# Other places in SBUF for the operands of three matmul stages of a decoder layer

## The chip, the cores and the metric

The kernel runs on one core of one Trainium2 chip. The metric is the device time of one execution in microseconds. TensorE (PE) does the matmuls, VectorE (DVE), ScalarE (ACT) and GpSimd (POOL) the elementwise work, and SyncE (SP) issues most transfers. All operands of a matmul lie in SBUF, each in 128 partitions, and a tile is a stretch of bytes that has the same place in every partition.

## The reference

One hybrid decoder layer over 16 meta tokens and 1,024 tokens of width 1,024: a joint input projection, differential attention and an HGRN2 recurrence side by side, an output projection, and a convolutional FFN with 2 x 2,816 channels.

```python
a = rmsnorm(h, ln_mix_pre[l])
proj = a @ w_in[l]
dq, dk, dv, hq, hf, hi, hg = jnp.split(proj, SPLITS, axis=-1)
y_diff = diff_attention(dq, dk, dv, ...)
y_hgrn = hgrn2(hq, hf, hi, hg, lb_all[l], hgrn_gnorm[l])
mix = jnp.concatenate([y_diff, y_hgrn], axis=-1) @ w_out[l]
h = h + rmsnorm(mix, ln_mix_post[l])
a = rmsnorm(h, ln_ffn_pre[l])
y = conv_ffn(a, w_ffn_up[l], ffn_conv_w[l], ffn_conv_b[l], w_ffn_down[l])
h = h + rmsnorm(y, ln_ffn_post[l])
```

`conv_ffn` is `u = a @ w_up`, a causal depthwise convolution of width 3 over the tokens, `gelu(gate) * up`, and `@ w_down`. Everything is float32.

## The kernel before, in words

A float32 product is made of three fp32r matmuls. Each operand is split into a high part (rounded to fp32r) and a low part (the rest), and hi x hi, hi x lo and lo x hi are summed in PSUM. A matmul has a stationary tile of 128 x 128, which TensorE loads for it, and a streamed operand of up to 512 columns. The load for one matmul runs while the one before it streams. TensorE's instructions stand in the order in which the code issues them (`manual_schedule`).

Three stages matter here.

The *projections* (`proj_step`, L243, and the class `Kinds`, L892) have weights stationary (`wh`, `wl`) and stream the normalized activations `ahi` and `alo`, tiles of 8 x 1,152 columns, over three groups of token blocks: 272, 384 and 384 columns. `place(t)` (L46) says at which column a token stands; after the first group it leaves 16 columns (64 bytes) free. `gap(...)` takes some bytes that nobody uses, so that the tiles behind it move up. The projections of one head run between the small matmuls of attention or HGRN of another.

The *up stage* (`unit`, L1396) uses one level of Strassen's scheme in Winograd's form: per 128 channels seven products `mm(0)` to `mm(6)`, each over four blocks of 128 rows and for two parts of the tokens, p = 0 with 258 columns and p = 1 with 256. The weights `uh`, `ul` are stationary. The streamed tiles `t0_0` to `t0_6` and `t1_0` to `t1_6` are made once, before the loop, by `t_split` and `t_sums`; each holds four high blocks and then four low ones. L1411 streams the high block against high weights, L1412 the low block against high weights, L1413 the high block against low weights. A block of 258 columns is 1,032 bytes long, so the low half starts 4,128 bytes behind the high one, which is 32 bytes modulo 512, and each next block 8 bytes further modulo 512; with 256 columns (1,024 bytes) all blocks of a tile have one place modulo 512. The loop over `ft` runs the 258-wide and the 256-wide product of each j in turn, 12 matmuls each, 21 times seven. The first unit (`plain_unit`, L1378) does without Strassen and uses four of the tiles.

The *down stage* (`operands`, L1500, `mms`, L1580) also has seven products. Here the gated activations are stationary: `gh` and `gl`, tiles of 512 columns in a ring of four buffers each (pool `down`), of which matmul m takes columns 128 m to 128 m + 127. The weights `wh`, `wl` (512 columns) are streamed: L1585 `wh` against `gh`, L1586 `wl` against `gh`, L1587 `wh` against `gl`. Each step of a product takes one buffer of each and does 12 matmuls, three for each of four PSUM banks.

The output projection between them streams weights too (L1031 to L1035), against tiles of the mixed heads; the tile `m7` holds the eighth row block, whose products have `pz` as output where they are added last (`out_last`, L1081).

All weight tiles, `wh` and `wl` of every stage, stand at 480 modulo 512 in each of their buffers, but for the third projection's first tiles (`w3`, taken from the attention's pool).

Of the kernel before, what the change touches and what calls it, by code (L numbers as in the profile page):

```python
# [9 lines left out]
F32 = mybir.dt.float32  # L10
F32R = mybir.dt.float32r
# [6 lines left out]
P = 128  # L18
# [19 lines left out]
def start(i):  # L38
    return 0 if i == 0 else META + P * (i - 1)
# [4 lines left out]


def place(t):  # L46
    return t + (0 if t < start(3) else 16)


class Ordered:  # L50
# [40 lines left out]
def layer_kernel(ctx: ExitStack, tc: tile.TileContext, x, meta, table, lbl, gpre, gpost, win,  # L91
# [7 lines left out]
    def pool(name, bufs, side="left", space=None):  # L99
        kw = {"side": side} if space is None else {"space": space}  # L100
        cm = tc.tile_pool(name=name, bufs=bufs, reuse_waits="tile", **kw)
        return cm, cm.__enter__()
# [70 lines left out]
    mx_cm, mxp = pool("mix", 1)  # L173

    MIX = {"X0": 2064, "X1": 2176, "X2": 2080}
# [4 lines left out]
    def gap(where, name, n):  # L180
        where.tile([P, n // 4], F32, tag=name, name=name, bufs=1)
# [11 lines left out]
                         m[:, l, off:off + P * n].bitcast(F32).rearrange("p (b c) -> p b c", c=P))  # L193

    at_cm, atp = pool("at", 1)
    gap(atp, "edge", 64)
    ahi, alo = (atp.tile([P, KD, P * NBLK], F32R, tag=t, name=t) for t in ("ahi", "alo"))

    last_load, lows = [], []
# [837 lines left out]
    def meta_part(py, wo, full):  # L1037
        for k in range(KD - 1):
            hi, lo = wo[k]
            both = [(34, hi), (2, lo)]  # L1040
            if k == KD - 2:
                both.reverse()
            for i, (r, w) in enumerate(both):
                T.matmul(py[:r], m0[:, 2 * k:2 * k + r], w, start=(k == 0 and i == 0), stop=(r == 34 and k == KD - 2))
                yield 216
            if k == 0 and full:
                yield from out_part(m0_7, py, wo[KD - 1:], range(1), False, False)
# [18 lines left out]
    def second_load(i):  # L1066
        blocks[i] = block_tile(1, i)
        block_load(blocks[i], i, 0, 4)
        block_load(blocks[i], i, 4, 7 if i == 1 else 8)
# [7 lines left out]
    def y0_gain(p):  # L1077
        r = tok(p)[0]
        return G.tensor_tensor(y0[:r, p], y0[:r, p], gpo0[:r], op=ALU.mult)
# [40 lines left out]
    def ps_b(name):  # L1120
        return pp.tile([P, 512], F32, tag="b", name=name)
# [80 lines left out]
    def load_xh(i):  # L1202
        r = tok(i)[0]
        if i:
            xhs[i] = qp.tile([P, D], F32, tag="xh", name=f"xh{i}")
        else:
            xhs[i], xhs["sum"] = xh0[:, :D], xh0[:, D:]
        SY.dma_start(xhs[i][:r], meta[14:16, :] if i == 0 else x[P * (i - 1): P * i, :])
# [51 lines left out]
    def t_tiles(p, j, where, tag):  # L1260
        tag, n, off = (tag + (8 * WN[p], 0)[len(tag) - 1:])[:3]
        both = where.tile([P, n], F32R, tag=tag, name=f"t{p}_{j}")[:, off:off + 8 * WN[p]].rearrange("p (a c) -> p a c", a=8)
        return both[:, 0:4], both[:, 4:8]

    def t_split(p, j, src, where, *tag):
        hi, lo = t_tiles(p, j, where, tag)
        marks["cast"] = A.copy(hi, src)
        marks["low"] = V.tensor_tensor(lo, src, hi.bitcast(F32), op=ALU.subtract)
        tt[p][j] = (hi, lo)

    def quarter(p, j):
        n = WN[p]
        a, c = {0: (0, 0), 7: (0, n), 4: (4, 0), 6: (4, n)}[j]
        return at2[p][:, a:a + 4, c:c + n]

    def t_sums(p, where, last):
        b11, b12, b21, b22 = (quarter(p, j) for j in (0, 7, 4, 6))
        cast, low = marks["quarters"]
        with tc.issue_after(low.ins) if p else nullcontext():
            V.tensor_tensor(b11, b12, b11, op=ALU.subtract)  # L1280
        V.tensor_tensor(b12, b22, b12, op=ALU.subtract)
        V.tensor_tensor(b22, b22, b11, op=ALU.subtract)
        for j, b in ((1, b22), (2, b11), (3, b12)):
            if p == 0:
                gap(where, f"gap4{j}", 128 if j == 1 else 192)
            with nullcontext() if p or j == 1 else tc.issue_after(cast.ins):
                with nullcontext() if p or j == 1 else tc.issue_after(low.ins):
                    t_split(p, j, b, where, f"t{p}_{j}")
        V.tensor_tensor(b21, b21, b22, op=ALU.subtract)
        with nullcontext() if p else tc.issue_after(cast.ins):  # L1290
            with nullcontext() if p else tc.issue_after(low.ins):
                t_split(p, 5, b21, *last)

    def run(*args):
        for _ in out_part(*args):
            pass
# [4 lines left out]
    for i in range(1, NBLK):  # L1301
        py = ps_b(f"py1_{i}")
        if i >= 3:
            marks["gain"] = y0_gain(i)
        if i == 1:
            load_xh(1)
            load_xh(0)
        if i + 1 < NBLK:
            for n in range(i + 1 if i < 6 else i + 2, min(i + 2 if i < 5 else i + 3, NBLK)):
                second_load(n)  # L1310
            load_xh(i + 1)
        run(blocks[i], py, wo, range(4), True, False)
        if i == 3:
            trans(1)
        run(blocks[i], py, wo, range(4, 7 if i == 1 else 8), False, i > 1)
        if i > 3:
            trans(i - 2)
        if i == 5:
            trans(0)
        if i == 1:  # L1320
            pm = ps_b("py1_0")
            for _ in meta_part(pm, wo, True):
                pass
            for p in range(3):
                out_last(p)
            run(k7(1), py, wo[KD - 1:], range(1), False, True)
            post(1, py)
            ysum = xhs.pop("sum")
            for l in range(2):
                A.copy(ysum[:2, 512 * l:512 * l + 512], pm[32 * l:32 * l + 2])  # L1330
            G.tensor_tensor(ysum[:2, :512], ysum[:2, :512], ysum[:2, 512:], op=ALU.add)
            for p in (3, 4):
                out_last(p)
            continue
        post(i, py)
        if i == 2:
            post(0, ysum[:, :512], ysum[:, 512:])
        if i == 5:
            t_split(0, 0, quarter(0, 0), ep, "e0")
            t_split(0, 4, quarter(0, 4), ep, "e1")  # L1340
        if i == 7:
            with tc.issue_after(marks["scale"].ins), tc.issue_after(marks["normed"].ins):
                t_split(0, 7, quarter(0, 7), mxp, "X2", MIX["X2"])
        if i == 8:
            t_split(0, 6, quarter(0, 6), mxp, "X1", MIX["X1"], 16)
        if i in (2, 3):
            for p in (1 + 2 * i, 2 + 2 * i):
                out_last(p)
# [6 lines left out]
    def outputs(ft, p):  # L1355
        if ft == 1 or ft and ft % 2 == NF % 2:
            if p == 0:
                return [dn.tile([P, 2 * WN[0]], F32, tag="gk", name=f"{t}{ft}_{p}") for t in ("ug", "uu")]
            return [dn.tile([P, 512], F32R, tag=g, name=f"{t}{ft}_{p}").bitcast(F32) for g, t in (("gh", "ug"), ("gl", "uu"))]
        return [xup.tile([P, 2 * WN[0]], F32, tag=t, name=f"{t}{ft}_{p}") for t in ("ug", "uu")]  # L1360

    def conv(ft, p, side, u):
# [94 lines left out]
    t_sums(0, tp, (mxp, "X2", MIX["X2"], 16))  # L1457
    close(a_cms.pop())
    t2_cm, t2p = pool("tsplit2", 1)
    gap(t2p, "gap2", 64)  # L1460
    p1 = plain_unit(1, ps_b)
    for j in range(4):
        with tc.issue_after(wo_low[5].ins), tc.issue_after(wo_low[4].ins):
# [6 lines left out]
    dn_cm, dn = pool("down", 4, "right")  # L1470
# [29 lines left out]
    def operands(pr, k, loaded=None):  # L1500
        ga, gb, gc, gs = (keep[nm][:, k] if keep else None for nm in ("ga", "gb", "gc", "gs"))
        if pr == 1:
            a = loaded[0] if loaded else g_in(k, 0, "1")
        elif pr == 2:
            SY.dma_start(gb, g_src(k + NH, 0))
            a = gb
        elif pr == 5:
            a = gs
        elif pr == 6:
            V.tensor_tensor(gs, gs, ga, op=ALU.add)  # L1510
            a = gs
        elif pr == 3:
            V.tensor_tensor(gb, gs, gb, op=ALU.subtract)
            a = gb
        elif pr == 7:
            V.tensor_tensor(ga, gc, ga, op=ALU.subtract)
            a = ga
        else:
            a = g_in(k + NH, 1, "4")
        b = loaded[1] if loaded else w_in(pr, k)  # L1520
        nm = f"{pr}_{k}"
        gh = dn.tile([P, 512], F32R, tag="gh", name=f"gh{nm}")
        gl = dn.tile([P, 512], F32R, tag="gl", name=f"gl{nm}")
        split(gh, gl, a, V)
        wh = wp.tile([P, 512], F32R, tag="wh", name=f"wh{nm}", bufs=4)
        wl = wp.tile([P, 512], F32R, tag="wl", name=f"wl{nm}", bufs=4)
        split(wh, wl, b, V)
        return gh, gl, wh, wl
# [210 lines left out]
```

## Time and profile before

| | us |
|---|---|
| median of the runs | 1275.93 (1275.89 to 1275.97) |
| profiled execution, whole | 1276.64 |
| its span, first to last instruction | 1274.9 |
| projections, attention, HGRN | from the start to 497 |
| output projection, residual, norm | 497 to 617 |
| first FFN unit | 617 to 643 |
| up stage | 643 to 1055 |
| down stage and tail | 1055 to the end |

The page and the views give, for a group of instructions, its source line, engine, operation and tiles, written out<-in without buffer numbers, how many there are, their busy time and the mean length of one. The length of a matmul runs from its start to its last result, so that neighbours overlap; the pace is the distance of two starts. TensorE's clock was granted in full, 0.999.

### The profile page before, as it was taken

To read this page: it belongs to the slowest core of one execution; us is meant where nothing else is said; L and a number is where in the kernel's file an instruction comes from. 1 tells how busy PE (TensorE), PEld (TensorE's weight loads), DVE (VectorE), ACT (ScalarE), POOL (GpSimd) and SP (SyncE) were. 2 spreads that over 40 slices of the span, in tenths; PEclk is the share of its full clock that TensorE was granted. 3 is DMA by queue.
4 is the path that set the end of the run, shared out by engine and by line. 5 is a ranking of instruction groups with operands and counts; after the bars stand their busy time and mean duration, and the time that the engine had idled before them with its cause. 6 is when DMAs were issued, how large, how long until landed. Compare 5 with 4: busy or idle time off the path is not lost.

```text
span 1274.9 us, 26032 instructions
## 1 busy us (share of the span) xinstructions
PE 1256.4 (99%) x10154; PEld 1172.8 (92%) x10154; DVE 914.5 (72%) x1489; ACT 687.2 (54%) x1635; POOL 507.8 (40%) x390
## 2 busy tenths in 40 slices
PE   8999999999999999999999999999999999999997
PEld 7999999999999998778899999999999998888886
DVE  7665646565656564557899888898898877797586
ACT  8475466546654754356764544445535445564554
POOL 5231423241323311353067676676776731020121
PEclk9999999999999999999999999999999999999999
DMA  7335555273734633688322221322222238955363
GB/s 260 96 60 131 89 140 96 80 146 93 132 94 79 125 81 119 217 268 276 129 67 68 92 87 64 100 76 75 92 76 84 75 113 262 355 180 173 91 215 124
DMA packets 116561, 165.04 MB, mean 129 GB/s; under 512 B 10115, under 2 KB 57539, under 8 KB 116438
## 3 DMA queue, kind: packets, MB, share of 16 engines
q1 hardware_dynamic: 93206, 151.84, 37.1%
q0 software_dynamic: 23232, 11.54, 7.7%
q8 instruction: 80, 1.31, 0.4%
q14 instruction: 43, 0.35, 0.1%
HBM read 134.24 MB, written 52.17 MB: 146 GB/s over the span
## 4 chain that ended last, share of the span: by engine, by line
PE 48%; DVE 3%; DMA 1%; ACT 1%; issue 1%; POOL 1%; DVEq 0%; SPq 0%; ACTq 0%; POOLq 0%
PE pd L1586 5%; PE pd L1587 5%; PE pd L1585 5%; PE pb L1412 4%; PE pb L1411 4%; PE pb L1413 4%; PE pa L1412 3%; PE pc L1412 3%; PE pa L1411 3%; PE pc L1411 3%; PE pc L1413 3%; PE pa L1413 3%; PE pq L1390 1%; PE pq L1389 1%; PE pq L1391 1%
## 5 line engine op out<-in xcount | busy, mean ns | idle before, releaser
L1412 PE MATMUL pb<-t,uh 128*128 128x258 f32 x504 | 140.9, 280 | 0.3 <-DVE t L58 0.3
L1411 PE MATMUL pb<-t,uh 128*128 128x258 f32 x504 | 140.5, 279 | 0.8 <-DVE u L58 0.8
L1413 PE MATMUL pb<-t,ul 128*128 128x258 f32 x504 | 140.1, 278 | 0.0
L1586 PE MATMUL pd<-wl,gh 128*128 128x512 f32 x308 | 120.3, 391 | 0.9 <-DVE wl L58 0.9
L1587 PE MATMUL pd<-wh,gl 128*128 128x512 f32 x308 | 120.0, 389 | 0.0
L1585 PE MATMUL pd<-wh,gh 128*128 128x512 f32 x308 | 119.9, 389 | 0.0
L58 DVE SCALAR_TENSOR_TENSOR c<-uu,cwt,c 128x514 f32<-128x514 f32 (+1 forms) x88 | 107.0, 1215 | 0.0
L58 DVE SCALAR_TENSOR_TENSOR c<-ug,cwt,c 128x514 f32<-128x514 f32 (+1 forms) x88 | 101.4, 1153 | 0.0
L1411 PEld LDWEIGHTS pb<-t,uh 128*128 128x128 f32 x504 | 94.8, 188 | 1.0 <-DVE u L58 1.0
L1412 PEld LDWEIGHTS pb<-t,uh 128*128 128x128 f32 x504 | 94.8, 188 | 0.5 <-DVE t L58 0.5
L58 ACT ACTIVATE c<-c 128x514 f32<-128x514 f32 (+1 forms) x44 | 27.9, 634 | 124.7 <-DVE c L58 124.7
L1413 PEld LDWEIGHTS pb<-t,ul 128*128 128x128 f32 x504 | 94.8, 188 | 0.0
L1412 PE MATMUL pa<-t,uh 128*128 128x258 f32 (+1 forms) x336 | 93.9, 280 | 0.0
L1412 PE MATMUL pc<-t,uh 128*128 128x258 f32 (+1 forms) x336 | 93.9, 279 | 0.0
L58 POOL TENSOR_TENSOR ws<-ra,ra 128x512 f32<-128x512 f32 x42 | 69.2, 1648 | 61.8 <-DMA ra<-in_wup_dram 31.4
L1411 PE MATMUL pa<-t,uh 128*128 128x258 f32 (+1 forms) x336 | 93.6, 279 | 0.0
L1411 PE MATMUL pc<-t,uh 128*128 128x258 f32 (+1 forms) x336 | 93.6, 278 | 0.0
L1413 PE MATMUL pa<-t,ul 128*128 128x258 f32 (+1 forms) x336 | 93.4, 278 | 0.0
L1413 PE MATMUL pc<-t,ul 128*128 128x258 f32 (+1 forms) x336 | 93.4, 278 | 0.0
L58 POOL TENSOR_TENSOR ul<-ws,uh 128x512 fp32r<-128x512 f32 x42 | 69.1, 1646 | 60.0 <-PE pa L1413 44.2
L58 POOL TENSOR_TENSOR c<-c,c 128x514 f32<-128x514 f32 (+1 forms) x44 | 67.9, 1543 | 52.6 <-ACT c L58 49.2
L58 DVE TENSOR_TENSOR ul<-ra,uh 128x512 fp32r<-128x512 f32 x43 | 41.5, 966 | 46.6 <-POOL ul L58 46.6
(389 smaller groups left out, 4184.0 us busy)
## 6 DMA issues: line engine op xcount, KB each, us to landing
ra<-in_wup_dram SPq DMA_DIRECT2D x88, 256.0 KB, 2.6
mp<-msc SPq DMA_DIRECT2D x23, 512.0 KB, 5.6
tsc<-in_wdown_dram SPq DMA_DIRECT2D x44, 256.0 KB, 4.8
wi<-tsc SPq DMA_DIRECT2D x44, 256.0 KB, 3.1
gi<-gsc SPq DMA_DIRECT2D x33, 256.0 KB, 4.0
wi<-in_wdown_dram SPq DMA_DIRECT2D x33, 256.0 KB, 5.0
gsc<-c SPq DMA_DIRECT2D x22, 257.0 KB, 2.1
tsc<-in_wdown_dram POOLq DMA_DIRECT2D x22, 256.0 KB, 7.0
```

The costliest lines, as they stand in the source:

```text
L58: ins = call(*args, **kw)
L1389: T.matmul(pt, hi[:, s], th[:, k], start=(kh + k == 0), stop=False)
L1390: T.matmul(pt, hi[:, s], tl[:, k], start=False, stop=False)
L1391: T.matmul(pt, lo[:, s], th[:, k], start=False, stop=(kh == 1 and k == 3))
L1411: T.matmul(pt, hi[:, s], th[:, k], start=(first and k == 0), stop=False, skip_group_check=True)
L1412: T.matmul(pt, hi[:, s], tl[:, k], start=False, stop=False, skip_group_check=True)
L1413: T.matmul(pt, lo[:, s], th[:, k], start=False, stop=(k == 3), skip_group_check=True)
L1585: T.matmul(py, gh[:, s], wh, start=(k == 0 and pr not in (3, 7)), stop=False, skip_group_check=True)
L1586: T.matmul(py, gh[:, s], wl, start=False, stop=False, skip_group_check=True)
L1587: T.matmul(py, gl[:, s], wh, start=False, stop=(k == NH - 1), skip_group_check=True)
```

## The change

The instructions and their order are the same on all five engines. The change moves tiles within SBUF:

```diff
 def place(t):
-    return t + (0 if t < start(3) else 16)
+    return t + (0 if t < start(3) else 16 if t < start(6) else 32)
...
-    gap(atp, "edge", 64)
+    gap(atp, "edge", 96)
...
-                gap(where, f"gap4{j}", 128 if j == 1 else 192)
+                gap(where, f"gap4{j}", 160 if j == 1 else 256)
...
-            t_split(0, 6, quarter(0, 6), mxp, "X1", MIX["X1"], 16)
+            t_split(0, 6, quarter(0, 6), mxp, "X1", MIX["X1"], 8)
...
-            return [dn.tile([P, 512], F32R, tag=g, name=f"{t}{ft}_{p}").bitcast(F32) for g, t in (("gh", "ug"), ("gl", "uu"))]
+            return [dn.tile([P, 528], F32R, tag=g, name=f"{t}{ft}_{p}").bitcast(F32)[:, :512] for g, t in (("gh", "ug"), ("gl", "uu"))]
...
-    gap(t2p, "gap2", 64)
+    gap(t2p, "gap2", 416)
...
-        gh = dn.tile([P, 512], F32R, tag="gh", name=f"gh{nm}")
-        gl = dn.tile([P, 512], F32R, tag="gl", name=f"gl{nm}")
+        gh = dn.tile([P, 528], F32R, tag="gh", name=f"gh{nm}")[:, :512]
+        gl = dn.tile([P, 528], F32R, tag="gl", name=f"gl{nm}")[:, :512]
```

What comes of it, as the built programs have it: the streamed operand's place less the stationary tile's, modulo 512 bytes (for a 258-wide tile that of its first block; the next three stand 8, 16 and 24 further).

| stage | operand | matmuls | before | after |
|---|---|---|---|---|
| projections | group 1 (272 columns) | 648 | 192 | 224 |
| | group 2 (384) | 648 | 320 | 352 |
| | group 3 (384) | 648 | 320 | 416 |
| | the same against `w3` | 72 | 0, 128, 256 | 32, 160, 224, 288, 352 |
| up, 258 wide | `t0_1` high / low | 252 | 64 / 96 | 96 / 128 |
| | `t0_2` | 252 | 320 / 352 | 416 / 448 |
| | `t0_3` | 252 | 64 / 96 | 224 / 256 |
| | `t0_6` | 252 | 64 / 96 | 32 / 64 |
| | `t0_0`, `t0_5` | 504 | 64 / 96 | the same |
| | `t0_4` | 252 | 320 / 352 | the same |
| up, 256 wide | all seven | 1,764 | 192 or 448 | the same |
| down | `gh`, four buffers | 616 | 0 | 0, 448, 384, 320 |
| | `gl`, four buffers | 308 | 0 | 64, 128, 192, 256 |

In the down stage the streamed weights stay at 480 and the stationary buffers move: `gh` stands at 480, 32, 96 and 160, `gl` at 416, 352, 288 and 224. `t0_6` is also used by 24 matmuls of the first unit. The tiles of the output projection keep their places; there d is 0, and 128 for `m7`.

## The prediction

> **What bounds the kernel now.** I read the page first, then the busy time by stage, the waits of TensorE, and last the starts and durations of single matmuls.
>
> ```profile
> span 1274.9 us, 26032 instructions
> PE 1256.4 (99%) x10154; PEld 1172.8 (92%) x10154; DVE 914.5 (72%) x1489; ACT 687.2 (54%) x1635; POOL 507.8 (40%) x390
> 0.00:36.00 36.00, 31.04 (x184) 26.12 (x185) 26.57 (x48) 29.90 (x71) 18.39 (x27) 1.00 0.67 230
> 36.00:497.00 461.00, 460.71 (x4329) 445.99 (x4328) 270.39 (x606) 262.52 (x765) 134.51 (x130) 1.00 0.47 101
> 497.00:617.00 120.00, 116.89 (x980) 91.97 (x979) 74.89 (x102) 63.06 (x179) 46.33 (x36) 1.00 0.77 250
> 617.00:643.00 26.00, 25.47 (x216) 25.19 (x215) 24.19 (x24) 21.61 (x39) 0.00 (x0) 1.00 0.22 73
> 643.00:1055.40 412.40, 411.26 (x3530) 410.87 (x3530) 355.58 (x471) 200.92 (x366) 282.25 (x180) 1.00 0.26 84
> 1055.40:1275.00 219.60, 211.01 (x925) 172.68 (x923) 162.92 (x242) 109.19 (x219) 26.32 (x17) 0.99 0.60 198
> PE pg L835 <- DMA grow<-in_gpre_dram: 2.3, 1, 2.3
> PE pl L477 <- issue: 1.9, 1, 1.9
> ```
>
> In the windows the columns are the stretch, its length, then PE, weight loads, DVE, ACT and POOL busy (with counts), the granted clock, the DMA share and GB/s. The stretches are the opening, attention and HGRN with the projections, the output projection, the first FFN unit, the up stage, and the down stage with the tail. PE is busy 99% of the span at a granted clock of 0.99 to 1.00, and its longest single wait is 2.3 us. So TensorE's own pace sets the time: a nanosecond on each of a thousand matmuls is a microsecond at the end, and one on another engine is nothing.
>
> The change leaves every engine's instructions, their order and their waits as they were. Only places in SBUF move. The question is therefore whether a matmul of one shape takes another time when its streamed operand and its stationary tile stand otherwise to each other. I call d the place of the streamed operand less that of the stationary tile loaded beside it, modulo 512 bytes. The places are the built program's, and the table of the change has them.
>
> Matmuls overlap, so their pace is read from start to start. These rows are single matmuls: start, duration, line, tiles. The first pair is in the down stage, the second around one block of the output projection, then one 258-wide and one 256-wide group of the up stage, then a 384-wide and a 272-wide projection.
>
> ```profile
> 1082.82 0.39 PE L1585 MATMUL pd<-wh,gh 128*128 128x512 f32 x1
> 1085.54 0.39 PE L1585 MATMUL pd<-wh,gh 128*128 128x512 f32 x1
> 565.85 0.39 PE L1031 MATMUL pz<-woh,m 128*128 128x512 f32 x1
> 567.94 0.39 PE L1031 MATMUL pz<-woh,m 128*128 128x512 f32 x1
> 672.61 0.28 PE L1411 MATMUL pb<-t,uh 128*128 128x258 f32 x1
> 674.04 0.28 PE L1411 MATMUL pb<-t,uh 128*128 128x256 f32 x1
> 675.40 0.28 PE L1411 MATMUL pa<-t,uh 128*128 128x258 f32 x1
> 277.03 0.34 PE L248 MATMUL pi_dk<-ahi,wh_dk 128*128 128x384 f32 x1
> 279.11 0.34 PE L248 MATMUL pi_dk<-ahi,wh_dk 128*128 128x384 f32 x1
> 116.59 0.29 PE L250 MATMUL pi_hg<-alo,wh_hg 128*128 128x272 f32 x1
> 118.08 0.29 PE L250 MATMUL pi_hg<-alo,wh_hg 128*128 128x272 f32 x1
> ```
>
> Twelve steps lie between the rows of a pair, nine in the second. The paces are 2.72/12 = 226.7 ns in the down stage, 2.09/9 = 232.2 ns in that block, 1.43/12 = 119 ns at 258 columns, 1.36/12 = 113.3 ns at 256, 2.08/12 = 173.3 ns at 384 and 1.49/12 = 124 ns at 272.
>
> **The change, part by part.** The *down stage's stationary rows* come first: 924 matmuls, all at d = 0 before. Afterwards 152 keep 0 and 772 are spread over the seven other multiples of 64. The nearest rows are the block at 565.85. It streams the same kind of weights, at the same place, in the same shape; its stationary tile `m7` alone stands elsewhere, with d = 128, and its nine steps take 232.2 ns against 226.7. All its matmuls (`pz`) are longer than the down stage's (`pd`):
>
> ```profile
> L1586 PE MATMUL pd<-wl,gh 128*128 128x512 f32 x308 | 120.3, 391 | 0.9 <-DVE wl L58 0.9
> L1587 PE MATMUL pd<-wh,gl 128*128 128x512 f32 x308 | 120.0, 389 | 0.0
> L1585 PE MATMUL pd<-wh,gh 128*128 128x512 f32 x308 | 119.9, 389 | 0.0
> L1031 PE MATMUL pz<-woh,m x9: 392/395/404, 565.2 to 583.2; 128*128 128x512 f32 x8, 128*2 128x512 f32 x1
> L1033 PE MATMUL pz<-wol,m x9: 388/392/404, 565.4 to 583.5; 128*128 128x512 f32 x8, 128*2 128x512 f32 x1
> ```
>
> In the last two rows min/median/max stand behind the count. One d of seven is seen so. I take its price for all: 772 x 5.5 ns = +4.2 us. The low end is the shortest `pz` matmul, 388 ns against a mean of 389 to 391: 772 x -2 = -1.5 us. The high end charges all 924: +5.1 us.
>
> At this place a rule of the Trainium skill speaks against any price. Its page "SBUF — State Buffer", section "Who interferes with whom", gives TensorE two independent read ports, one for the streamed operand and one for weight loads, and says that it never waits on anyone. By that rule this term would be 0; the 232.2 ns row does not agree with it, though nine matmuls are few.
>
> *Four of the up stage's 258-wide tiles* (`t0_1`, `t0_2`, `t0_3`, `t0_6`). A tile holds a high and a low half, and the low half starts 32 bytes past the high one modulo 512. So the trace already has odd multiples of 32: L1411 and L1413 stream high halves (even multiples), L1412 low halves (odd ones). At 256 columns the halves share one d:
>
> ```profile
> L1412 PE MATMUL pb<-t,uh 128*128 128x258 f32 x252 | 71.3, 283 | 0.0
> L1411 PE MATMUL pb<-t,uh 128*128 128x258 f32 x252 | 71.0, 282 | 0.8 <-DVE u L58 0.8
> L1413 PE MATMUL pb<-t,ul 128*128 128x258 f32 x252 | 70.6, 280 | 0.0
> L1412 PE MATMUL pb<-t,uh 128*128 128x256 f32 x252 | 69.7, 276 | 0.3 <-DVE t L58 0.3
> L1411 PE MATMUL pb<-t,uh 128*128 128x256 f32 x252 | 69.5, 276 | 0.0
> ```
>
> With one d the lines are equal at 276. With two, the odd one takes 283 and the even ones 281 on average, so odd costs 2 ns and does not pay. The edit swaps the roles: 4 tiles x 4 blocks x 21 units = 336 triples, each with two streams made odd and one made even: 672 x 2 - 336 x 2 = +0.7 us. The low end is 0 or a little below, if the line's position makes the 2 ns; the high end, where these groups also upset the 256-wide ones, is a rival below.
>
> *Projection groups*: 2,016 matmuls, 1,344 at 384 columns and 672 at 272. d goes from 320 to 352 or 416, and from 192 to 224 (72 with the third weight tile come from and go to other such values). No row shows this shape at an odd multiple. The 2 ns above would make 2,016 x 2 = +4.0 us, its opposite -4.0 us. Since a 384-wide group keeps one d throughout, as the steady 256-wide ones do, I take a quarter of the upper price, +1.0 us. The high end is the 5.5 ns of the 512-wide block, 11 us; the low end is the first rival.
>
> The profiled execution took 1276.6 us in all, 1274.9 of it span. Its sum becomes 1276.6 + 4.2 + 0.7 + 1.0 = 1282.5 us. It lies 0.7 above the median of the runs, so the forecast is 1282 us, its own bounds 1277 to 1288. The copies that fill the moved tiles are as many and as large as before. They sit on DVE (72% busy), ACT and POOL, and even a slower one would find cover under PE.
>
> **Rivals.** *The odd multiples run evenly (not slower).* Paces per column differ: 113.3/256 and 226.7/512 are both 0.443 ns, 173.3/384 is 0.451, 124/272 is 0.456, 119/258 is 0.461. If the new places let the moved streams run at 0.443, a projection would take 170.0 and 120.4 ns, an up matmul 114.2. That is 1,344 x 3.3 + 672 x 3.6 + 1,008 x 4.8 = 4.4 + 2.4 + 4.8 = 11.6 us less. With the down stage unmoved it gives 1264 us, with its +4.2 us 1269. For it: uneven paces show that something in the order of 3 to 5 ns a matmul depends on more than width. Against it: L1412 at odd multiples is no faster.
>
> *Nothing happens.* Place has no price, and the 232.2 ns come from the short block being cut off from its like. The time is then 1276 us. The rule of the Trainium skill on the two ports, told above, would give this.
>
> *The up stage's 256-wide groups lose their rhythm.* The same shapes with the same d run slower in the first FFN unit:
>
> ```profile
> L1389 PE MATMUL pq<-t,uh 128*128 128x256 f32 x32 | 9.1, 284 | 0.0
> L1391 PE MATMUL pq<-t,ul 128*128 128x256 f32 x32 | 9.0, 281 | 0.0
> ```
>
> 281 against 276 ns, with places unchanged, means that a pace can lock in two ways. If the moved 258-wide groups, which come before each 256-wide one, push it to the slow way, 1,764 x 5 = +8.8 us come on top: 1291 us. Against it: the fast way held through 20 units and their stalls.
>
> *A pace without any loss.* If the new places took away whatever slows the streams, the moved matmuls would gain far more than 0.443 ns a column. They fill 1,344 x 173.3 + 672 x 124 + 1,008 x 119 + 924 x 226.7 ns = 646 us, so a gain of 25 us or more, 1250 us or less, needs 4% of each. The rows above differ by 2% at most between places, and the shortest `pz` matmul, 388 ns, is 0.3% under the mean of `pd`; so this has little chance. The Trainium skill's page "TensorE: Matmul & The Clock Gate", section "Back-to-back issue gap", states N/2.4 + 2.5 ns for back-to-back matmuls: an estimate by it is 215.8 ns at 512 and 162.5 at 384, and all moved streams at that pace would give 1237 us. No row of this case is as fast.
>
> *Much slower.* The unsteady price at the projections (11 us), the lost rhythm (8.8) and the down stage (5.1) together: +25 us, 1301. It needs all three.
>
> **How the numbers follow.** Chances: forecast 0.45, even odd multiples 0.20, nothing 0.17, lost rhythm 0.10, no loss 0.04, much slower 0.04. The range runs from 1266 to 1290 us: it holds the forecast and "nothing", most of the even case and about half of the lost rhythm, and leaves out some 0.2. 2% is 25.5 us, about what a measurement of this kernel can tell from no change. Only the last two cases reach it, the slow one at its edge; with something for a price that no row hints at I give 0.04 faster, 0.89 within, 0.07 slower. The forecast stays on the slow side of no change, well within.
>
> **What would show it.** Right: `pd` matmuls of 393 to 396 ns instead of 389 to 391, with paces near 232; L1411 and L1413 at 258 columns up by about 1 ns in the mean, L1412 down by one; steady 384-wide projections within 3 ns of 173.3; 256-wide groups still at 276; PE's waits as before. Wrong: `pd` at 389 (then "nothing" or the even case, told apart by whether the projections' 173.3 falls to 170), or 256-wide matmuls at 281 (lost rhythm). A forecast missed by over 15 us means a price of place far above any that these rows hold.

## The result and the profile after

The changed kernel takes 1284.52 us (median of 2 runs, 1284.36 to 1284.68) against 1275.93 before: a ratio of 1.0059, 95% interval 1.0042 to 1.0075, some 5 to 10 us more. The profiled executions differ by 8.0 us (1284.68 and 1276.64).

These are lines of the page, of the windows and of the waits of TensorE after the change. The borders of the windows stand at the same places of the program as in the windows before.

```profile
span 1282.9 us, 26032 instructions
PE 1264.8 (99%) x10154; PEld 1179.3 (92%) x10154; DVE 915.8 (71%) x1489; ACT 687.8 (54%) x1635; POOL 507.1 (40%) x390
36.00:499.50 463.50, 463.32 (x4330) 448.62 (x4330) 270.55 (x607) 262.98 (x766) 134.63 (x130) 1.00 0.46 100
499.50:618.90 119.40, 116.80 (x980) 91.95 (x979) 76.18 (x103) 63.03 (x179) 46.81 (x36) 1.00 0.77 252
618.90:644.20 25.30, 25.10 (x216) 24.82 (x215) 23.46 (x24) 21.14 (x39) 0.00 (x0) 1.00 0.18 67
644.20:1060.50 416.30, 414.74 (x3530) 414.34 (x3529) 356.05 (x471) 201.55 (x366) 280.96 (x180) 1.00 0.26 84
1060.50:1282.90 222.40, 213.60 (x925) 172.99 (x923) 163.16 (x242) 109.44 (x219) 26.31 (x17) 0.99 0.59 196
PE pg L835 <- DMA grow<-in_gpre_dram: 2.4, 1, 2.4
```

TensorE is busy for the same share of the span at the same granted clock, its longest wait is the same one, and DVE, ACT and POOL have the same busy time to 1.3 us. So the 8.0 us are TensorE's own. By stage, against the windows of before: projections 463.5 - 461.0 = +2.5, output projection 119.4 - 120.0 = -0.6, first FFN unit 25.3 - 26.0 = -0.7, up stage 416.3 - 412.4 = +3.9, down stage and tail 222.4 - 219.5 = +2.9 (the last window of before ended 0.1 us behind the span).

In the down stage, all three lines are longer (before: 391, 389, 389 for L1586, L1587, L1585). The second fence has the first matmul of five steps of 12 in a row, from the timeline.

```profile
L1586 PE MATMUL pd<-wl,gh 128*128 128x512 f32 x308 | 121.1, 393 | 1.4 <-DVE wl L58 1.3
L1585 PE MATMUL pd<-wh,gh 128*128 128x512 f32 x308 | 121.1, 393 | 0.0
L1587 PE MATMUL pd<-wh,gl 128*128 128x512 f32 x308 | 120.4, 391 | 0.0
```

```profile
1090.72 0.40 PE L1585 MATMUL pd<-wh,gh 128*128 128x512 f32 x1
1093.49 0.40 PE L1585 MATMUL pd<-wh,gh 128*128 128x512 f32 x1
1096.27 0.39 PE L1585 MATMUL pd<-wh,gh 128*128 128x512 f32 x1
1099.00 0.39 PE L1585 MATMUL pd<-wh,gh 128*128 128x512 f32 x1
1101.75 0.40 PE L1585 MATMUL pd<-wh,gh 128*128 128x512 f32 x1
```

The steps take 2.77, 2.78, 2.73 and 2.75 us. They use the four buffers in turn, with d (`gh`/`gl`) of 448/128, 384/192, 0/256 and 320/64; before, a step took 2.72. Over the whole stage the median step of each has a pace of 231.2, 231.3, 227.6 and 228.9 ns. So the ring of four buffers has not one price but four.

In the up stage the moved groups are the 258-wide ones, yet the 256-wide ones, whose place against the weights is as it was, are slower. First the groups by form, then the start of each product in one round of the loop: `t0_6`, `t1_6`, `t0_0`, `t1_0`, `t0_1`, `t1_1`, then `t0_3`, `t1_3` and the next.

```profile
L1411 PE MATMUL pb<-t,uh 128*128 128x258 f32 x252 | 71.4, 284 | 0.8 <-DVE u L58 0.8
L1412 PE MATMUL pb<-t,uh 128*128 128x258 f32 x252 | 71.1, 282 | 0.0
L1411 PE MATMUL pb<-t,uh 128*128 128x256 f32 x252 | 69.9, 277 | 0.0
L1411 PE MATMUL pc<-t,uh 128*128 128x256 f32 x168 | 46.9, 279 | 0.0
```

```profile
702.46 0.28 PE L1411 MATMUL pc<-t,uh 128*128 128x258 f32 x1
703.90 0.28 PE L1411 MATMUL pc<-t,uh 128*128 128x256 f32 x1
705.31 0.28 PE L1411 MATMUL pa<-t,uh 128*128 128x258 f32 x1
706.74 0.28 PE L1411 MATMUL pa<-t,uh 128*128 128x256 f32 x1
708.15 0.28 PE L1411 MATMUL pb<-t,uh 128*128 128x258 f32 x1
...
715.24 0.28 PE L1411 MATMUL pb<-t,uh 128*128 128x256 f32 x1
716.60 0.28 PE L1411 MATMUL pa<-t,uh 128*128 128x258 f32 x1
```

The starts of `t1_6`, `t0_0`, `t1_0` and `t0_1` in the kernel before:

```profile
701.98 0.28 PE L1411 MATMUL pc<-t,uh 128*128 128x256 f32 x1
703.34 0.28 PE L1411 MATMUL pa<-t,uh 128*128 128x258 f32 x1
704.77 0.28 PE L1411 MATMUL pa<-t,uh 128*128 128x256 f32 x1
706.13 0.28 PE L1411 MATMUL pb<-t,uh 128*128 128x258 f32 x1
```

`t1_6` takes 705.31 - 703.90 = 1.41 us and `t1_0` 708.15 - 706.74 = 1.41, which is 117.5 ns a matmul; before, each took 1.36, 113.3 ns, as `t1_3` still does. `pc` holds products 2 and 6, and its 256-wide mean of 279 is between the 276 of before and the 281 of the first unit's rows.

These are the mean paces, worked out from all starts in the two traces (distances across a wait left out):

| ns from start to start | before | after |
|---|---|---|
| projections, 272 columns | 123.8 | 125.6 |
| projections, 384 columns | 173.5 | 175.2 |
| first unit, 256 columns | 117.8 | 113.4 |
| up, 258 columns | 119.5 | 119.9 |
| up, 256 columns | 113.3 | 114.9 |
| of these `t1_6`, `t1_0`, `t1_1` | 113.3, 113.5, 113.3 | 118.0, 117.6, 115.4 |
| down, 512 columns | 226.6 | 229.7 |

The paces in the experiments below are worked out in the same way, from the one trace that each kernel has, and "stage" is the distance of the first matmuls of two stages, for the down stage that from its first matmul to its last.

### The profile page after: what moved, and what is told of

It is laid out like the page before. It is cut to its first block, busy times and chain, and to the rows that moved or that the text cites. A ratio compares the mean times of both kernels' runs of the same rounds, so it can differ in the third digit from the quotient of the medians.

```text
span 1282.9 us, 26032 instructions
## 1 busy us (share of the span) xinstructions
PE 1264.8 (99%) x10154; PEld 1179.3 (92%) x10154; DVE 915.8 (71%) x1489; ACT 687.8 (54%) x1635; POOL 507.1 (40%) x390
## 4 chain that ended last, share of the span: by engine, by line
PE 43%; DVE 4%; DMA 4%; ACT 2%; issue 1%; SPq 0%; POOL 0%; DVEq 0%; ACTq 0%
PE pb L1411 4%; PE pb L1412 4%; PE pb L1413 4%; PE pd L1586 4%; PE pd L1587 4%; PE pd L1585 4%; PE pc L1413 3%; PE pc L1411 3%; PE pc L1412 3%; PE pa L1411 3%; PE pa L1412 3%; PE pa L1413 3%; DMA gi<-gsc 2%; DVE xh L58 1%; DVE t L58 1%
## 5 line engine op out<-in xcount | busy, mean ns | idle before, releaser
L1411 PE MATMUL pb<-t,uh 128*128 128x258 f32 x504 | 141.3, 280 | 0.8 <-DVE u L58 0.8
L1412 PE MATMUL pb<-t,uh 128*128 128x258 f32 x504 | 141.0, 280 | 0.8 <-DVE t L58 0.8
L1586 PE MATMUL pd<-wl,gh 128*128 128x512 f32 x308 | 121.1, 393 | 1.4 <-DVE wl L58 1.3
L1585 PE MATMUL pd<-wh,gh 128*128 128x512 f32 x308 | 121.1, 393 | 0.0
L1587 PE MATMUL pd<-wh,gl 128*128 128x512 f32 x308 | 120.4, 391 | 0.0
L1412 PEld LDWEIGHTS pb<-t,uh 128*128 128x128 f32 x504 | 95.1, 189 | 1.0 <-DVE t L58 1.0
L1411 PEld LDWEIGHTS pb<-t,uh 128*128 128x128 f32 x504 | 94.8, 188 | 1.0 <-DVE u L58 1.0
L58 POOL TENSOR_TENSOR c<-c,c 128x514 f32<-128x514 f32 (+1 forms) x44 | 72.0, 1637 | 57.3 <-ACT c L58 54.6
L1412 PE MATMUL pc<-t,uh 128*128 128x258 f32 (+1 forms) x336 | 94.3, 281 | 0.0
L1411 PE MATMUL pc<-t,uh 128*128 128x258 f32 (+1 forms) x336 | 94.3, 281 | 0.0
L1412 PE MATMUL pa<-t,uh 128*128 128x258 f32 (+1 forms) x336 | 94.3, 281 | 0.0
L1411 PE MATMUL pa<-t,uh 128*128 128x258 f32 (+1 forms) x336 | 94.1, 280 | 0.0
L58 POOL TENSOR_TENSOR ws<-ra,ra 128x512 f32<-128x512 f32 x42 | 64.1, 1526 | 61.6 <-DMA ra<-in_wup_dram 44.3
```

Source lines behind the costliest of these rows:

```text
L58: ins = call(*args, **kw)
L1411: T.matmul(pt, hi[:, s], th[:, k], start=(first and k == 0), stop=False, skip_group_check=True)
L1412: T.matmul(pt, hi[:, s], tl[:, k], start=False, stop=False, skip_group_check=True)
L1585: T.matmul(py, gh[:, s], wh, start=(k == 0 and pr not in (3, 7)), stop=False, skip_group_check=True)
L1586: T.matmul(py, gh[:, s], wl, start=False, stop=False, skip_group_check=True)
L1587: T.matmul(py, gl[:, s], wh, start=False, stop=(k == NH - 1), skip_group_check=True)
```

## The experiments

**Place alone.** A program that does nothing but matmuls, 24 in a row for each place and width, so that no other engine and no transfer is at work beside them.

```python
for name, ds, lift in (("a", up, 0), ("b", mixed, 0), ("c", mixed, 32)):
    for n in (512, 384, 272, 258, 256):
        for d in ds:   # 0 to 496 in steps of 16
            ...
            nc.tensor.matmul(pt[:, :n], w[:, o:o + P], s[:, s0:s0 + n], start=(k == 0), stop=(k == RUN - 1))
```

> The layer is left out; the kernel only runs matmuls of 512, 384, 272, 258 and 256 columns, 24 in a row for each place d of the stream less the stationary tile (0 to 496 in steps of 16 bytes), in rising order, in a mixed order, and in the mixed order with both operands 32 bytes further. Theory of relative place: the pace at 512 columns is 226.7 ns at d = 0 and some 230 to 233 at most other d, 173 at 384 for d = 320 and about 3 more for d = 352, and it is the same with both operands moved by 32. Rival of the absolute place: moving both by 32 changes the pace as much as moving one. Rival of independent ports: one pace for each width, whatever d is.

The page's lines of the engines and of the DMA (in 40 slices of the span), then stretches of the timeline, each of which is one row of matmuls in a run: at 512 columns d = 256, 64 and 128; at 384 d = 320 and 352; at 256 d = 192 and 64.

```profile
PE 1778.5 (99%) x11520; PEld 1676.3 (93%) x11520; DVE 1.1 (0%) x2; ACT 4.3 (0%) x5; POOL 0.2 (0%) x4
...
DMA  0000000000000000000000000000000000000002
```

```profile
653.54 3.11 PE L73 MATMUL b<-s,w 128*128 128x512 f32 x13
631.25 3.13 PE L73 MATMUL b<-s,w 128*128 128x512 f32 x13
698.10 3.18 PE L73 MATMUL b<-s,w 128*128 128x512 f32 x13
869.16 2.59 PE L73 MATMUL b<-s,w 128*128 128x384 f32 x14
894.58 2.46 PE L73 MATMUL b<-s,w 128*128 128x384 f32 x13
1185.91 1.75 PE L73 MATMUL b<-s,w 128*128 128x256 f32 x14
1117.96 1.81 PE L73 MATMUL b<-s,w 128*128 128x256 f32 x14
```

A row lasts from its first start to its last end, so the length of one matmul has to come off. At 512 columns that is 0.39 us: (3.11 - 0.39)/12 = 226.7 ns, and the row at d = 128 is 0.07 us longer for the same twelve steps, 6 ns each. At 256 columns the row at 64 is 0.06 us longer over thirteen steps, 4.6 ns each. From all starts, the last 12 distances of each row in order "b":

```text
d mod 256      0      32     64     96     128    160    192    224
512 columns  226.7  233.3  228.8  233.3  232.8  234.3  233.3  233.3
384 columns  173.3  176.7  173.3  176.7  175.6  173.3  174.6  173.3
256 columns  120.0  116.7  117.8  120.0  118.4  119.0  113.3  118.0
```

Three things follow. The place matters with nothing else at work. It is the relative place that matters, as far as one shift can show it: order "c", both operands 32 bytes on, has the same pace as "b" everywhere to 0.5 ns. And d + 256 gives the pace of d, except at 6 of the 80 pairs of "b", so the period is 256 bytes. But place is not all: with the places taken in another order ("a") 39 of 160 rows settle at another pace, at 512 columns and d = 0 for instance at 232.2 instead of 226.7. What ran before decides which of two steady paces a row falls into.

**One part at a time.** Each part of the change alone, against the kernel before.

```diff
 # projections alone
-    return t + (0 if t < start(3) else 16)
+    return t + (0 if t < start(3) else 16 if t < start(6) else 32)
-    gap(atp, "edge", 64)
+    gap(atp, "edge", 96)
 # up stage alone
-                gap(where, f"gap4{j}", 128 if j == 1 else 192)
+                gap(where, f"gap4{j}", 160 if j == 1 else 256)
-            t_split(0, 6, quarter(0, 6), mxp, "X1", MIX["X1"], 16)
+            t_split(0, 6, quarter(0, 6), mxp, "X1", MIX["X1"], 8)
-    gap(t2p, "gap2", 64)
+    gap(t2p, "gap2", 416)
 # down stage alone
-        gh = dn.tile([P, 512], F32R, tag="gh", name=f"gh{nm}")
+        gh = dn.tile([P, 528], F32R, tag="gh", name=f"gh{nm}")[:, :512]
...
```

Projections:

> The projections' part of the change alone. Theory of relative place: the trace of the changed kernel has group 2 (d = 352) 3.1 ns slower per matmul, group 3 (d = 416) 0.7, group 1 (d = 224) 1.9, together 2.5 us later at the end of the attention stage; so 1278.4 us, ratio 1.0020, with the up and down stages as before. Rival, that the parts act through each other: within 0.7 us of 1275.9, or over 1281.

Up stage:

> The up stage's four tiles alone. Theory of relative place with a rhythm that persists: the 256-wide groups t1_0 and t1_6, which do not move, run at 118 ns again instead of 113.3, t1_1 at about 115, the 258-wide ones 0.3 ns slower; the up stage takes 3.9 us more and the first unit 0.7 us less, in all 1279.1 us. Rival, only the moved tiles pay: 258-wide groups alone change, +0.6 us, 1276.5 us.

Down stage:

> The down stage's stationary rows alone. Theory of relative place: 12-matmul steps of 227.6, 228.9, 231.2 and 231.2 ns for the four buffers, in the mean 229.7 instead of 226.6, +3.1 us: 1279.0 us, with the up stage's 256-wide groups at 113.3. Rival, the down stage's loss comes from the changed up stage before it: 1276 us.

| alone | ratio to before | its stage | what runs at another pace |
|---|---|---|---|
| projections | 1.0022 (1.0014 to 1.0031) | +2.3 us | 272 at d = 224: 125.6; 384 at 352: 176.5, at 416: 174.0 |
| up stage | 1.0031 (1.0019 to 1.0043) | +3.9 | 256 columns 114.9, first unit 113.6 |
| down stage | 1.0014 (1.0005 to 1.0023) | +2.2 | 512 columns 229.7 |

Each part costs, and each only in its own stage: the other stages keep the paces of before. The ratios add up to 1.0067, within the interval of the whole change. The matmuls of the down stage slow down by 924 x 3.1 ns = 2.8 us, the stage by 2.2. The rest comes out of its stalls: what its distances of over 260 ns have beyond the pace adds up to 2.2 us before and 1.6 here. The up stage is the dearest part, with half as many matmuls moved as in the projections (1,008 and 2,016).

**All rows of the down stage at one place.** One gap more in the pool moves all `gh` and `gl` alike, by 128 bytes in one kernel and 256 in the other.

```diff
-        if (ft, p) == (1, 0):
-            gap(dn, "gap7", 384)
+        if ft == 1:
+            gap(dn, f"gap7{p}", (384, 128)[p])   # the other kernel: (384, 256)[p]
```

> The kernel before with all stationary rows of the down stage at d = 128, none changing from step to step. Theory of relative place, by the sweep (232.5 to 232.8 ns at 512 columns): 924 x 5.9 ns = +5.5 us, 1281.4 us. Rival, it is the change of place from step to step that costs, since each change breaks the rhythm: one place throughout runs at 226.7 ns, 1276 us.

> The kernel before, with all stationary rows of the down stage moved 256 bytes, so that the streamed weights stand 256 past them throughout (before: 0). Nothing else is moved. The sweep had 226.7 ns at 0 and at 256, and in the changed kernel the buffers at 0 and 256 ran at 227.6. Theory (only the place modulo 256 counts): a pace of 226.6 in the down stage, as before, and a ratio of 1.000. Rival (any move away from the weights' own place modulo 512 costs): as at 128, a pace near 232.7, down stage 216, ratio 1.0026.

The groups of L1586, from 128 and from 256; the last number is the idle time ahead of them:

```profile
L1586 PE MATMUL pd<-wl,gh 128*128 128x512 f32 x308 | 121.8, 396 | 0.1
```

```profile
L1586 PE MATMUL pd<-wl,gh 128*128 128x512 f32 x308 | 120.3, 391 | 1.4 <-DVE wl L58 1.4
```

At 128: pace 232.75 ns, stage 216.1 us (+4.1), ratio 1.0026 (1.0016 to 1.0035). At 256: pace 226.59, ratio 1.0004 (0.9992 to 1.0016), no change. So moving rows costs nothing by itself, and the cost does not need a change of d from step to step; standing 128 bytes off costs 6 ns a matmul, as with the matmuls alone. Of the 924 x 6.1 = 5.7 us only 4.1 show in the stage. The other 1.6 come out of its stalls, which add up to 0.6 us here against 2.2 before; they alone make the stage 212.0 to 213.9 us long in the kernels of this study whose rows stay at d = 0. The 1.0 ns that the buffer at 0/256 costs in the changed kernel is no price of its own place, since 0 and 256 throughout both run at 226.6; what makes it, the steps around it perhaps, was not tested.

**Other odd multiples for the projections.** All groups at 160 or 224, with no columns left free between them.

```diff
-    return t + (0 if t < start(3) else 16)
+    return t + 0
-    gap(atp, "edge", 64)
+    gap(atp, "edge", 32)
```

> The kernel before with the projection groups at other odd multiples of 32: group 1 at d = 160, groups 2 and 3 at d = 224. Theory of relative place, by the sweep's paces for these places (123.3 and 173.3 ns, the same as at 192 and 320): 1276 us, ratio 1.000 within 0.001. Rival, odd multiples of 32 as such cost 1 to 3 ns a matmul: 1278 to 1281 us.

The ratio is 1.0017 (1.0007 to 1.0026), the stage +1.7 us, the paces 124.6 at 272 columns and 174.7 at 384, against 123.8 and 173.5 before. The expectation of no loss was wrong, and the rival's number came true. The matmuls alone do reach 173.3 at d = 224, but in two of the three orders only after some seven of them, which run at 174 to 179. In the kernel the projections come in short runs between small matmuls, which can end before that. The traces bear this out when the distances of each unbroken run are sorted by their place in it: at 384 columns the first five are 175.6 ns in the mean and those from the ninth on 173.3 (before: 173.6 and 173.3), at 272 columns 125.2 and 123.2 (before: 124.0 and 123.4). So a place has two prices here, its steady pace and how long it takes to fall into step. An odd multiple as such, the rival, would not come down to 173.3. With the projections' part of the change alone, the groups at 352 stay at 176.8 to 177.0 from the first distances to the last: there it is the steady pace that costs.

**The up stage's pattern alone.** Twelve matmuls of 258 columns and twelve of 256 in turn, nothing else; the 256-wide ones always at 192 or 448, the 258-wide ones at 32 first places.

```python
for n, place in ((258, lambda k, l: d + step * k + low * l), (256, lambda k, l: e)) * REPS:
    ...
    for k in range(4):
        for c, (h, l) in enumerate(((0, 0), (0, 1), (1, 0))):
            nc.tensor.matmul(pt[:, :n], w[:, o:o + P], s[:, a:a + n], start=(k + c == 0), stop=(k + c == 5))
```

> The layer is left out; the kernel only runs the up stage's pattern, 12 matmuls of 258 columns (four blocks, each 8 bytes further, low half 32 bytes further, high, low, high half streamed) and then 12 of 256 columns with d = 192 or 448, five times for each place d of the first block (0 to 248 in steps of 8), and then with blocks that stand alike, and with 16 and 64 bytes in place of 8 and 32. Theory of a rhythm that is set by what ran before: the 256-wide groups, whose own places never change, run at 113.3 ns behind some d of the 258-wide group and at 117 to 120 behind others; at d = 64 as in the kernel before both 119.5 and 113.3. Rival, each group has the pace of its own place: the 256-wide groups at 113.3 throughout.

```text
first d of the 258-wide      8      16     32     48     64     96     200    240
258 columns, ns            118.3  118.8  118.6  119.4  120.1  120.7  118.8  121.2
256 columns, ns            113.9  117.8  113.6  117.8  114.3  115.4  119.0  117.7
```

The 256-wide groups never moved (the eight columns are for 192; 448 gave the same), and their pace runs from 113.6 to 119.0, by where the groups ahead of them stand. The same program also ran blocks that stand alike, and steps of 16 and 64 bytes in place of 8 and 32: the 256-wide groups went from 113.3 to 118.2 there. That a group has the pace of its own place is refuted. The numbers at 64 also differ from the kernel, which has 119.5 and 113.3 there; why is open.

**Which tile throws the others out.** First the changed kernel with `t0_6` alone put back, then the kernel before with `t0_6` alone moved.

```diff
 # from the changed kernel
-            t_split(0, 6, quarter(0, 6), mxp, "X1", MIX["X1"], 8)
+            t_split(0, 6, quarter(0, 6), mxp, "X1", MIX["X1"], 16)
 # from the kernel before
-            t_split(0, 6, quarter(0, 6), mxp, "X1", MIX["X1"], 16)
+            t_split(0, 6, quarter(0, 6), mxp, "X1", MIX["X1"], 8)
```

> The changed kernel with tile t0_6 alone back at its old place. Theory: t0_6 is what throws the 256-wide groups of t1_6 and, over t0_0, of t1_0 out of step, so both run at 113.3 ns again, and the up stage is 2.4 to 2.9 us shorter than in the changed kernel: 1282 us. The 256-wide groups of the first unit go back to 117.8. Rival, t0_1 to t0_3 are what does it: t1_6 and t1_0 stay at 118 and the time at 1284.5 us less at most 0.3.

> The kernel before with t0_6 alone at the changed kernel's place (32 past the weights instead of 64), nothing else moved. Theory (t0_6 alone throws t1_6 and t1_0 out, and puts the first unit's 256-wide groups at the quick pace): t1_6 and t1_0 near 118, t1_1 between 113.3 and 114.3, up stage +2.2 to +2.8 us, first unit -0.7 us, ratio 1.0012 to 1.0018. Rival (it takes the other moved tiles too): t1_6 and t1_0 stay at 113.3 to 113.5, up stage as before, ratio 0.9995 with the first unit's gain.

Put back: up stage 413.5 us, `t1_6` at 113.3, `t1_0` at 113.5, `t1_1` at 114.3, first unit back at 117.8; ratio 1.0038 (1.0023 to 1.0053). Moved alone: up stage 415.1 us (+2.7), first unit -0.7, ratio 1.0015 (1.0005 to 1.0026), and in the timeline `t1_6`, `t0_0`, `t1_0`, `t0_1`, `t1_1` and the next start at

```profile
701.24 0.28 PE L1411 MATMUL pc<-t,uh 128*128 128x256 f32 x1
702.66 0.28 PE L1411 MATMUL pa<-t,uh 128*128 128x258 f32 x1
704.09 0.28 PE L1411 MATMUL pa<-t,uh 128*128 128x256 f32 x1
705.50 0.28 PE L1411 MATMUL pb<-t,uh 128*128 128x258 f32 x1
706.94 0.28 PE L1411 MATMUL pb<-t,uh 128*128 128x256 f32 x1
708.30 0.28 PE L1411 MATMUL pc<-t,uh 128*128 128x258 f32 x1
```

`t1_6` takes 1.42 us and `t1_0` 1.41, `t1_1` 1.36 again. So one moved tile slows two whose place against the weights is as it was, 504 matmuls by 4.4 ns on average = 2.2 us, and only two: behind `t0_0`, between them, the pace is still slow, behind `t0_1` it is quick again. The other three moved tiles are left with 413.5 - 412.4 = 1.1 us.

**Three tiles at 32.** `t0_1`, `t0_2`, `t0_3` at 32 modulo 256, a place that looked good in the pattern alone. The first kernel has only the first line of the edit; the second has both.

```diff
-                gap(where, f"gap4{j}", 128 if j == 1 else 192)
+                gap(where, f"gap4{j}", 352 if j == 1 else 192)
-    gap(t2p, "gap2", 64)
+    gap(t2p, "gap2", 352)
```

> The kernel before, with three of the up stage's 258-wide tiles (t0_1, t0_2, t0_3) moved so that they stand 32 past the weights modulo 256 instead of 64. Nothing else is moved. By the pattern of 258-wide and 256-wide groups alone the pair 32 / 192 was the quickest but one: 118.6 and 113.6 ns, against 120.1 and 114.3 at 64. The kernel before has about 119.5 and 113.3 there. Theory 1 (the pattern's paces carry over): 756 matmuls 0.9 ns quicker and the 756 behind them 0.3 ns slower, 0.5 us in all, so a ratio of 0.9996, no change that shows. Theory 2 (whether the 256-wide tiles keep the quick pace is decided by the neighbours in this kernel, as t0_6 at 32 threw t1_6 and t1_0 out of it): t1_1, t1_2 or t1_3 go to 117 to 118, 252 matmuls and 1.1 us for each, 2 to 4 us in all, ratio 1.0015 to 1.003.

> As three_32, which also moved t1_1, t1_2 and t1_3 (from 192 to 416, 160 modulo 256) and so changed two things at once: here the gap behind the sums makes up for it, and only t0_1, t0_2 and t0_3 stand elsewhere than before, 32 past the weights modulo 256 instead of 64. Theory 1 (the 256-wide tiles' own place made three_32 slow): t1_1 to t1_3 back at 113.3 to 113.6, up stage within 0.5 us of before's 412.4, ratio 1.000. Theory 2 (258-wide neighbours at 32 throw the 256-wide groups behind them out of the quick pace, as t0_6 does in the changed kernel): t1_1, t1_2 or t1_3 at 117 to 118, 1.1 us for each, up stage 413.5 to 416, ratio 1.001 to 1.003.

The first expectation was wrong in saying that nothing else moves: without the second line `t1_1`, `t1_2` and `t1_3` shift as well, to 416. That kernel (up stage 416.4 us, those tiles at 120.1, 117.1 and 117.2, ratio 1.003, 1.002 to 1.0041) does not tell the two theories apart. The second does. Its starts of `t1_0`, `t0_1`, `t1_1` and `t0_2`, and then of `t0_4`, `t1_4`, `t0_5`:

```profile
706.76 0.28 PE L1411 MATMUL pa<-t,uh 128*128 128x256 f32 x1
708.12 0.28 PE L1411 MATMUL pb<-t,uh 128*128 128x258 f32 x1
709.56 0.28 PE L1411 MATMUL pb<-t,uh 128*128 128x256 f32 x1
710.97 0.28 PE L1411 MATMUL pc<-t,uh 128*128 128x258 f32 x1
...
716.68 0.28 PE L1411 MATMUL pa<-t,uh 128*128 128x258 f32 x1
718.11 0.28 PE L1411 MATMUL pa<-t,uh 128*128 128x256 f32 x1
719.52 0.28 PE L1411 MATMUL pb<-t,uh 128*128 128x258 f32 x1
```

`t1_0` takes 1.36 us, then `t1_1` 1.41 and `t1_4` 1.41, though `t0_4` ahead of it did not move. By all starts `t1_1` to `t1_4` run at 117.8 to 118.0 and the others at 113.3 to 113.5; the 258-wide groups are at 119.6, against 119.5 before. The up stage takes 417.5 us, +5.1, more than theory 2 had expected, since four groups went and not one to three, and 1,008 x 4.6 ns = 4.6 us of it come from 256-wide tiles whose place against the weights is as it was. Ratio 1.0046 (1.0031 to 1.0061). The pattern's numbers did not carry over to the kernel; that a tile at 32 throws the next 256-wide group out of step, until some later group brings it back, did.

None of these versions beats the kernel before. Its places already have the quickest steady paces that the matmuls alone showed at 512, 384 and 256 columns; at 272 columns the place of before, 192, settled at 123.3, the quickest, in one order and at 126.7 in the two others, and at 258 there was a quicker one (116.7 ns at d = 16), but the pattern that starts at 16 had 118.8 and 117.8.

## Why the prediction was right, and where it was not

The forecast was 1282 us, and 1284.5 was measured, within the range. That nothing but places changes, that TensorE's pace is therefore all, and that places cost something but less than a hundredth, held. The terms of the sum did less well, and that their total came so near is partly luck. The projections and the up stage cost 4.7 us more than their terms, the down stage 1.3 less by the windows, and the output projection and the first unit, for which no term stood, were 1.3 shorter.

*Down stage, +4.2 predicted, +2.8 by the paces, +2.2 to +2.9 by the stage.* The mechanism was right, the size was not. The price of 5.5 ns, read from nine `pz` matmuls at d = 128, is right for that place: 6.1 ns over a whole stage. The lengths set beside it showed nothing of it: the 357 `py` matmuls of the output projection at d = 0 are 396 ns long on average, the 24 of `pz` at d = 128 395. Their paces did, 228.6 against 232.9. What failed was "I take its price for all": of the seven new places 256 is free and 64 and 320 cost 2 ns. The four buffers cost 1.0, 2.3, 4.6 and 4.7 ns over 226.6, 3.1 on average. The `pd` lengths came to 391 to 393 ns, not 393 to 396.

*Four up tiles, +0.7 predicted, +3.9 measured in the up stage.* For the moved 258-wide groups the price was about right: their pace rose from 119.5 to 119.9, 1,764 x 0.34 ns = +0.6 us, and of the `pb` lines L1411 rose from 282 to 284 while L1412 fell from 283 to 282. But this is a mean over unlike tiles: `t0_1` to `t0_3` rose by 0.8 to 1.1 ns, `t0_6` by 0.2, and `t0_0`, which did not move, fell by 0.4. The rule behind the price, that an odd multiple costs 2 ns, is not borne out: alone, 258 columns ran at 120.0 at 32 and 96, and at 119.4 or 122.2 at 64. What failed outright is that the 256-wide ones were kept out of the forecast, as a rival that takes all or nothing. They account for 1,764 x 1.6 ns = +2.9 us. The argument against it, "the fast way held through 20 units and their stalls", looked at stalls; what throws a group out is where the streams ahead of it stand. Nor does it happen to all seven: `t1_6` and `t1_0` go fully, `t1_1` in part. The first unit is the other side of the same thing: its 256-wide groups went from the slow pace to the quick one, 96 x 4.4 ns = -0.4 us of its -0.7.

*Projections, +1.0 predicted, +2.5 in the whole change, +2.3 alone.* The mechanism was open, and "a quarter of the upper price" was too little: the price was 1.8 ns at 272 columns and 1.7 at 384, near the 2 ns of the upper end. For all 2,016 that would be 3.5 us; the stage shows 2.5, and where the rest went was not traced. Every odd place tried in the kernel cost 0.5 to 3 ns on average, but not for being odd: the matmuls alone settle at 176.7 at 352, and at 173.3 at 416 and 224.

*Output projection, nothing predicted, -0.6.* Its length runs from 119.5 to 122.7 us in the kernels above, in which nothing of it moved, so this is no effect of the change.

*The rivals.* "Odd multiples run evenly" fell: no moved stream ran at 0.443 ns a column. "Nothing happens" fell with the first experiment. The rule of the Trainium skill behind it ("SBUF — State Buffer", section "Who interferes with whom"), that the read ports of TensorE are independent, would have d make no difference. These runs do not agree with it: with no other engine at work the pace at 512 columns goes from 226.7 to 236.7 ns by the relative place of the two operands. "A pace without any loss" had no support in any run: no mean pace was quicker than 226.6 ns at 512 columns and 113.3 at 256. "Lost rhythm" happened for two to three tiles of seven.

What stays open: what in TensorE or SBUF depends on d. The runs show the period, that both operands have to move against each other, and that the pace can lock in more than one way, but not the cause.

## What to carry to other kernels

Where TensorE is the bound, the place of a streamed operand against its stationary tile modulo 256 bytes is worth some per cent of a matmul: look for it in the distances of starts, and measure it per width and in the kernel's own sequence, since runs of one place alone predicted the 512-wide stage at one place but not the alternating one. In short runs the first few matmuls count too, as they can be slower than the steady pace. When one group's operand is moved, read the pace of the groups behind it too. A row of the trace gives the price of its own place alone: here a ring of buffers at four places had four prices.

## What the runs showed of the hardware

Two steady paces can hold at the same places. In the last kernel (three tiles at 32) all operands of the first unit lie at the same addresses as before, and its 256-wide groups ran at 113.4 ns there and at 117.8 before. The row of the first unit's line shows it, from before and then from that kernel (min/median/max of both widths):

```profile
L1389 PE MATMUL pq<-t,uh x64: 277/281/366, 617.5 to 642.6; 128*128 128x258 f32 x32, 128*128 128x256 f32 x32
```

```profile
L1389 PE MATMUL pq<-t,uh x64: 276/277/367, 619.2 to 643.6; 128*128 128x258 f32 x32, 128*128 128x256 f32 x32
```

What tipped it there is not known; in the three other kernels that had the quick pace `t0_6`, which runs shortly ahead, was moved. In the up stage's pattern alone, where each place is repeated five times, the 256-wide groups behind a first place of 112 took 117.6, 113.2, 117.6, 113.2 and 117.6 ns in turn, with nothing changed between the repeats.

The period of 256 bytes was also unexpected: the prediction reckoned d modulo 512, and the down stage with its rows moved by 256 ran as before.
